# Gated linear attention inside 128 tokens: two coarse levels as rectangles, the fine levels as 32 by 32 diagonal blocks

## The chip, the core and the metric

The kernel runs on one core of a Trainium2 chip. The core has a matrix engine (TensorE, PE in the profile, with PEld for its weight loads), a vector engine (VectorE, DVE), a scalar engine (ScalarE, ACT), GpSimd (POOL) and SyncE (SP), which issues the large transfers. Each engine runs its own queue of instructions in order. The metric is the device time of one execution in microseconds: 1452.02 us, the median of three runs (1451.77 to 1452.31).

## The reference

The program is two blocks on 256 tokens of width 1024. The first block has two layers, each a mixer of three parts (sparse attention, gated linear attention, spatial gating) and a feed-forward part; the second block has banded attention and a mixture of 32 experts. The change touches only the gated linear attention, once in each of the two layers. It has 4 heads, 32 key channels and 64 value channels a head:

```python
def gla_mixer(q, k, v, a_lr, r, w_up, b_up, norm_g):
    ...
    g = jax.nn.log_sigmoid((a_lr @ w_up + b_up).astype(f32)).reshape(B, S, H, DK) / GLA_TAU
    ...
        bcum = jnp.cumsum(gc, axis=2)
        o_inter = jnp.einsum('bhck,bhkv->bhcv', qc * jnp.exp(bcum), state)
        diff = bcum[:, :, :, None, :] - bcum[:, :, None, :, :]
        decay = jnp.exp(jnp.where(causal[None, None, :, :, None], diff, -jnp.inf))
        attn = jnp.einsum('bhik,bhjk,bhijk->bhij', qc, kc, decay)
        o_intra = jnp.einsum('bhij,bhjv->bhiv', attn, vc)
    ...
    o = rmsnorm(o, norm_g) * jax.nn.silu(r.astype(f32)).reshape(B, S, H, DV)
```

So each pair of a query token and an earlier key token has a weight: the sum over 32 channels of q times k times the decay of that channel between the two tokens.

## The kernel before, in words

**The heads.** The kernel does the linear attention in two halves of 128 tokens (`tb`) instead of chunks of 64, and makes the weights inside a half by levels. At level s (64, 32, 16, 8, 4, 2, 1) the half is cut into blocks of 2s tokens; every query in a block's upper s tokens meets every key in its lower s tokens, and the decay is split at the middle of the block: the query carries the factor from the middle to itself, the key the factor from itself to the middle. A last level is the diagonal, where there is no decay. `_tables` (L75) makes the matrix of ones that sums the gates for all levels (`decay`), and the masks; `t_gla` (L1205) makes the exponentials `ex` and multiplies q and k into them. Any pair of tokens belongs to just one level.

`heads(hp)` (L1266) is started for two pairs of heads. Each of the eight levels is a full 128x128 product per head and half, with 32 channels on the rows of the matrix engine: four bursts of two levels (L1267 to L1282), 16 matmuls a pair in each, into two banks of PSUM, a bank for each head of the pair. After a burst, two predicated copies on DVE (L1285 to L1291), each 128 partitions by 512, put the places of one level into `at`. At the end two matmuls a pair make the weights between the two halves, and ACT copies them out. When both pairs are done, `t_gla` multiplies the weights with v, normalises and gates; its root is a power on POOL (`grs`), and a product with the norm's gains on POOL follows.

**What sets the order.** The large products with weights ("dense" here) run on the matrix engine as one stream: each weight tile of 128 rows is split into a high and a low part, by a cast on ACT (`whi`) and a subtraction on DVE (`wlo`), and multiplied three times. A scheduler (`step`, L443; `tick`, L466) places everything else between these products: it keeps a modelled clock for each engine, charges each instruction a price (`price`, L262), and lets the generators of the mixers go on one `yield` at a time, by rank, where their inputs are ready by the model. `heads` has rank 7 (L43). The order of all instructions is thereby fixed when the program is built. A change in what `heads` issues, or in its prices, moves its neighbours in all queues.

The neighbours of `heads` are, in each layer: the spatial gating (its norm is on DVE, an operation on 128x256), the compressed keys and values (`t_cmp`, L832: two products on DVE that move them out of PSUM, then six additions of 64x240 on POOL), the rotation of q on POOL (`t_qk`, L1031) and the copy of its transpose on DVE in two halves, then the attention over selected blocks and the window (`t_branch`, L1103), and the output projection (`w_out`, L1507), which is dense. All instructions pass through a recording helper, so that the profile shows one line for all, L258; tiles tell them apart. `arena`, `arena_o` and `arena_y` are the working memory of the mixers, `psum` the accumulators, `raw` the slots into which weights arrive.

Of the kernel before, what the change touches and what calls it, by code (L numbers as in the profile page):

```python
# [13 lines left out]
P = 128  # L14
# [60 lines left out]
def _tables():  # L75
    f = np.float32
    p, j = np.arange(P), np.arange(P)
# [45 lines left out]
    u, t = p[:, None], p[None]  # L123
    lev = [np.where(u >= t + 1, 1.0, 0.0)]
# [5 lines left out]
    lev.append(np.where(u <= t, 1.0, 0.0))  # L130
    t1.add("decay", np.stack(lev, 1) / 16.0)
    t1.add("tril", (j[None] <= p[:, None]) * 1.0)
    masks = []
    for s in (64, 32, 16, 8, 4, 2, 1):
        q, k = p[None], p[:, None]
        masks.append((q // (2 * s) == k // (2 * s)) & (q % (2 * s) >= s) & (k % (2 * s) < s))
    masks.append(p[None] == p[:, None])

    t2 = Tables()
    for name, dil, back in (("dist0", 1, 128), ("dist1", 4, 128), ("dist2", 16, 128), ("dist3", 1, 127)):  # L140
# [4 lines left out]


TABLES, WHERE, MASKS = _tables()


# [421 lines left out]
class Kernel:  # L571
# [633 lines left out]
    def t_gla(self, l):  # L1205
        nc, S = self.nc, self.side
        yield from S.wait(("ar", l), ("gqk", l), ("gv", l), ("par", l))
        qk = self.zs["gqk"]
        b = yield from S.get(1)
# [7 lines left out]
        for tb in range(2):  # L1217
# [11 lines left out]
            out=g16.rearrange("p a b -> p (a b)"), in0=pg, scalar=0.0, in1=ab, op0=ALU.min, op1=ALU.subtract  # L1229
# [5 lines left out]
        ex = yield from self.ar.new(8, 2, P)  # L1235
        for half in range(2):
            for tb in range(2):
                b = yield from S.get(1)
# [6 lines left out]
                    out=ex[:, half * 4 : half * 4 + 4, tb, :],  # L1245
                    in_=self.ps(b[0]).rearrange("p (a t) -> p a t", a=4),
# [7 lines left out]
        for i, s in enumerate((64, 32, 16, 8, 4, 2, 1)):  # L1254
            for tb in range(2):
                e = ex[:, i + 1 - tb, tb, :].rearrange("p (n r s) -> p n r s", r=2, s=s)
# [6 lines left out]
        at = yield from self.ar.new(4, 2, P)  # L1263
        ax = yield from self.ar.new(4, P)
        nc.gpsimd.memset(at, 0.0)
        def heads(hp):  # L1266
            for lp in range(4):  # L1267
                bs = yield from S.get(2)
                for ll in range(2):
                    lev = lp * 2 + ll  # L1270
                    for tb in range(2):
                        for e in range(2):
                            r = slice((hp * 2 + e) * 32, (hp * 2 + e) * 32 + 32)
                            if lev < 7:
                                a = c = ex[r, lev + 1 - tb, tb, :]
                            else:
                                a, c = qk[r, 1, tb * P : tb * P + P], qk[r, 0, tb * P : tb * P + P]
                            o = (ll * 2 + tb) * P
                            self.nc.tensor.matmul(
                                self.ps(bs[e])[:, o : o + P], lhsT=a, rhs=c, start=True, stop=True,  # L1280
                                skip_group_check=True, tile_position=((hp * 2 + e) * 32, 0),
                            )  # L1282
                yield
                two = self.psum[:, bs[0] : bs[1] + 1 : bs[1] - bs[0], :]
                for ll in range(2):  # L1285
                    lev = lp * 2 + ll
                    nc.vector.copy_predicated(
                        out=at[:, hp * 2 : hp * 2 + 2].rearrange("p a b c -> p a (b c)").rearrange("p a (b c) -> p a b c", b=2),
                        mask=self.masks[:, lev * P : lev * P + P].unsqueeze(1).unsqueeze(1).to_broadcast([P, 2, 2, P]),
                        data=two[:, :, ll * 256 : ll * 256 + 256].rearrange("p a (b c) -> p a b c", b=2),  # L1290
                    )  # L1291
                S.put(bs)
                yield
            bs = yield from S.get(2)
            for e in range(2):
                r = slice((hp * 2 + e) * 32, (hp * 2 + e) * 32 + 32)
                self.nc.tensor.matmul(
                    self.ps(bs[e])[:, 0:P], lhsT=ex[r, 0, 0, :], rhs=ex[r, 7, 1, :], start=True, stop=True,
                    skip_group_check=True, tile_position=((hp * 2 + e) * 32, 0),
                )  # L1300
            yield
            two = self.psum[:, bs[0] : bs[1] + 1 : bs[1] - bs[0], 0:P]
            nc.scalar.copy(out=ax[:, hp * 2 : hp * 2 + 2, :], in_=two)
            S.put(bs)
            yield

        for hp in range(2):
            S.start(heads(hp), ("gla_heads", l, hp), BLOCKS[l]["rank"]["heads"])
        yield from S.wait(("gla_heads", l, 0), ("gla_heads", l, 1))
        self.ar.drop(ex, qk)  # L1310
        b = yield from S.get(1)
        ps = self.ps(b[0]).rearrange("p (t h d) -> p t h d", t=2, h=4)
        for h in range(4):
# [22 lines left out]
            out=srn, in0=srn, in1=self.gln[:, l, :].unsqueeze(1).to_broadcast([P, 8, 64]), op=ALU.mult  # L1336
# [1333 lines left out]
```

## Time and profile before

| | before |
|---|---|
| median of 3 runs | 1452.02 us |
| profiled execution, its own time | 1452.91 us |
| span in the trace | 1451.1 us |
| PE busy, its share of the span | 1311.3 us, 90% |
| DVE busy | 724.6 us, 50% |
| ACT busy | 559.8 us, 39% |
| POOL busy | 215.9 us, 15% |
| moved by DMA | 360.21 MB, mean 248 GB/s |

The span is what the trace covers from first to last instruction; the execution's own time is 1.8 us more. Busy shares are means over the whole program. In layer 0 the bursts of the heads begin at 72.51 us, the attention's first matmul is at 103.33, PE has nothing but dense work from 143.1 to the feed-forward part at 163.4. In layer 1 the same stages begin at 410.30, 440.90 and 480.0 us.

Times are in microseconds from the start of the span, unless marked ns. The trace counts two PE instructions for a matmul on full float32 inputs, and one for the split products.

### The profile page before, as it was taken

To read this page: it belongs to the slowest core of one execution; us is meant where nothing else is said; L and a number is where in the kernel's file an instruction comes from. 1 tells how busy PE (TensorE), PEld (TensorE's weight loads), DVE (VectorE), ACT (ScalarE), POOL (GpSimd) and SP (SyncE) were. 2 spreads that over 40 slices of the span, in tenths; PEclk is the share of its full clock that TensorE was granted. 3 is DMA by queue.
4 is the path that set the end of the run, shared out by engine and by line. 5 is a ranking of instruction groups with operands and counts; after the bars stand their busy time and mean duration, and the time that the engine had idled before them with its cause. 6 is when DMAs were issued, how large, how long until landed. Compare 5 with 4: busy or idle time off the path is not lost.

```text
span 1451.1 us, 23004 instructions
## 1 busy us (share of the span) xinstructions
PE 1311.3 (90%) x8865; PEld 977.9 (67%) x8865; DVE 724.6 (50%) x1521; ACT 559.8 (39%) x1175; POOL 215.9 (15%) x345
## 2 busy tenths in 40 slices
PE   9989999999999999999999999998887777867665
PEld 8777999988777899988989899885332311412111
DVE  5586677765588677765676655563210200110001
ACT  5526555554536555545564546541110100100001
POOL 2154111101055011102442302010000000000000
PEclk9998999999999999999999999999989979988888
DMA  9651556555524465557435354688999999999995
GB/s 342 193 170 47 162 179 199 167 195 177 178 96 147 131 189 183 186 188 225 152 94 169 117 163 141 220 327 354 419 420 420 421 421 420 420 421 421 421 419 211
DMA packets 155076, 360.21 MB, mean 248 GB/s; under 512 B 8752, under 2 KB 98352, under 8 KB 130768
## 3 DMA queue, kind: packets, MB, share of 16 engines
q1 hardware_dynamic: 152928, 354.81, 66.8%
q0 software_dynamic: 1248, 3.11, 0.7%
q8 instruction: 71, 1.16, 0.3%
q10 hardware_dynamic: 784, 0.76, 0.2%
q14 instruction: 45, 0.37, 0.1%
HBM read 357.60 MB, written 1.05 MB: 247 GB/s over the span
## 4 chain that ended last, share of the span: by engine, by line
PE 41%; DMA 22%; DVE 3%; ACT 2%; POOL 1%; issue 1%; POOLq 0%; DVEq 0%; SPq 0%; ACTq 0%
PE psum L258 41%; DMA raw<-in_w_e_up_dram 8%; DMA raw_left<-in_w_e_down_dram 3%; DMA arena_y<-in_w_e_up_dram 3%; DMA raw<-in_w_e_down_dram 3%; DMA raw_right<-in_w_e_up_dram 3%; DMA raw_right<-in_w_e_down_dram 1%; DMA raw_left<-in_w_e_up_dram 1%; DVE arena L258 1%; ACT whi L258 1%; ACT arena L258 1%; DVE wlo L258 1%; POOL arena L258 1%; DVE arena_o L258 0%; ACT arena_o L258 0%
## 5 line engine op out<-in xcount | busy, mean ns | idle before, releaser
L258 DVE TENSOR_TENSOR wlo<-raw,whi 128x512 fp32r<-128x512 f32 (+3 forms) x552 | 397.2, 727 | 260.5 <-ACT whi L258 249.4
L258 ACT CAST whi<-raw 128x512 fp32r<-128x512 f32 (+3 forms) x552 | 332.8, 606 | 344.6 <-PE psum L258 274.4
L258 PE MATMUL psum<-h_hi,whi 128*128 128x256 f32 x1040 | 297.8, 286 | 3.0 <-ACT whi L258 3.0
L258 PE MATMUL psum<-h_lo,whi 128*128 128x256 f32 x1040 | 291.6, 280 | 0.1
L258 PE MATMUL psum<-h_hi,wlo 128*128 128x256 f32 x1040 | 290.2, 279 | 0.0
L258 PEld LDWEIGHTS psum<-h_hi,whi 128*128 128x128 f32 x1040 | 195.8, 188 | 10.1 <-issue 4.8
L258 PEld LDWEIGHTS psum<-h_lo,whi 128*128 128x128 f32 x1040 | 196.2, 189 | 0.9 <-issue 0.5
L258 PEld LDWEIGHTS psum<-h_hi,wlo 128*128 128x128 f32 x1040 | 196.0, 188 | 0.2 <-DVE wlo L258 0.2
L258 PE MATMUL psum<-raw,arena 128*32 128x512 f32 x608 | 164.0, 672 | 19.1 <-DMA raw<-in_w_e_up_dram 12.6
L258 PE MATMUL psum<-arena 64*128 64x128 f32 (+10 forms) x752 | 160.1, 418 | 21.6 <-DVE arena L258 8.2
L258 PE MATMUL psum<-whi,h_hi 128*128 128x256 f32 (+3 forms) x448 | 145.8, 325 | 1.4 <-ACT arena_o L258 1.1
L258 PE MATMUL psum<-whi,h_lo 128*128 128x256 f32 (+3 forms) x448 | 138.3, 309 | 0.0
L258 PE MATMUL psum<-wlo,h_hi 128*128 128x256 f32 (+3 forms) x448 | 138.3, 309 | 0.0
L258 PEld LDWEIGHTS psum<-arena 64*128 64x128 f32 (+4 forms) x752 | 73.1, 175 | 69.8 <-issue 23.7
L258 DVE SCALAR_TENSOR_TENSOR arena<-arena,psum 128x256 f32<-128x256 f32 (+2 forms) x36 | 17.8, 517 | 201.7 <-ACT arena L258 198.8
L258 PEld LDWEIGHTS psum<-raw,arena 128*32 128x32 f32 x608 | 34.4, 121 | 99.8 <-issue 60.3
L258 PE MATMUL psum<-raw_left,arena 128*32 128x512 f32 x400 | 81.2, 712 | 20.9 <-DMA raw_left<-in_w_e_gate_dram 14.8
L258 POOL TENSOR_TENSOR arena<-arena 128x512 f32<-128x512 f32 (+2 forms) x46 | 49.0, 1074 | 295.3 <-DVE arena L258 289.0
L258 PEld LDWEIGHTS psum<-whi,h_hi 128*128 128x128 f32 x448 | 85.3, 190 | 11.0 <-issue 4.4
L258 PEld LDWEIGHTS psum<-wlo,h_hi 128*128 128x128 f32 x448 | 85.4, 191 | 4.6 <-issue 1.4
L258 PEld LDWEIGHTS psum<-whi,h_lo 128*128 128x128 f32 x448 | 85.2, 190 | 4.5 <-DVE h_lo L258 0.2
L258 DVE COPY arena<-psum 128x384 f32<-128x384 f32 (+6 forms) x60 | 32.6, 543 | 108.0 <-ACT arena L258 95.7
(247 smaller groups left out, 1761.5 us busy)
## 6 DMA issues: line engine op xcount, KB each, us to landing
raw<-in_w_e_up_dram SPq DMA_DIRECT2D x32, 1024.0 KB, 19.8
raw<-in_w_in_dram SPq DMA_DIRECT2D x60, 512.0 KB, 4.9
raw<-in_w_e_gate_dram SPq DMA_DIRECT2D x24, 1024.0 KB, 19.8
raw<-in_w_gate_dram SPq DMA_DIRECT2D x44, 512.0 KB, 4.0
raw<-in_w_up_dram SPq DMA_DIRECT2D x44, 512.0 KB, 5.1
raw<-in_w_down_dram SPq DMA_DIRECT2D x20, 1024.0 KB, 5.2
raw_left<-in_w_e_gate_dram SPq DMA_DIRECT2D x20, 1024.0 KB, 19.9
raw<-in_w_e_down_dram SPq DMA_DIRECT2D x19, 1024.0 KB, 19.8
```

The costliest lines, as they stand in the source:

```text
L258: return f(*args, **kw)
```

## The change

The levels 64 and 32 become products of just the rectangles in which they count (64 by 64, and two of 32 by 32 a half), and ACT copies those to `at`. The five levels from 16 down and the diagonal lie wholly in the four diagonal blocks of 32 by 32 of a half; they become 32 by 32 products: 6 levels, 2 halves, 4 blocks and 2 heads, 96 matmuls for a pair of heads, all in one burst without a `yield`, into two banks. Six predicated copies of 128x128 a pair merge them by mask into a new tile `a32`, and four copies on ACT put its blocks onto the diagonal of `at`. The products between the halves go into the second burst. The mask table goes from 128x256 words to 128x48.

```diff
     masks = []
-    for s in (64, 32, 16, 8, 4, 2, 1):
+    q, k = np.arange(32)[None], p[:, None] % 32
+    for s in (16, 8, 4, 2, 1):
         masks.append((q // (2 * s) == k // (2 * s)) & (q % (2 * s) >= s) & (k % (2 * s) < s))
-    masks.append(p[None] == p[:, None])
+    masks.append(q == k)
...
         nc.gpsimd.memset(at, 0.0)
+        a32 = yield from self.ar.new(4, 2, 32)
+        nc.gpsimd.memset(a32, 0.0)
+
         def heads(hp):
-            for lp in range(4):
-                bs = yield from S.get(2)
-                for ll in range(2):
-                    lev = lp * 2 + ll
-                    for tb in range(2):
+            def one(bank, n, rows, e, a, c):
+                h = hp * 2 + e
+                r = slice(h * 32, h * 32 + 32)
+                nc.tensor.matmul(
+                    self.ps(bank)[rows[0] : rows[1], n : n + c.shape[-1]], lhsT=a[r], rhs=c[r], start=True, stop=True,
+                    skip_group_check=True, tile_position=(h * 32, rows[0]),
+                )
+
+            hs = slice(hp * 2, hp * 2 + 2)
+            bs = yield from S.get(2)
+            for i in range(6):
+                lev = 2 + i
+                for tb in range(2):
+                    if lev < 7:
+                        a = c = ex[:, lev + 1 - tb, tb, :]
+                    else:
+                        a, c = qk[:, 1, tb * P : tb * P + P], qk[:, 0, tb * P : tb * P + P]
+                    for o in range(0, P, 32):
                         for e in range(2):
...
+                            one(bs[e], (i * 2 + tb) * 32, (o, o + 32), e, a[:, o : o + 32], c[:, o : o + 32])
+            yield
+            two = self.psum[:, bs[0] : bs[1] + 1 : bs[1] - bs[0], 0:384].rearrange("p e (i t c) -> p e i t c", i=6, t=2)
+            for i in range(6):
+                nc.vector.copy_predicated(
+                    out=a32[:, hs],
+                    mask=self.masks[:, i * 32 : i * 32 + 32].unsqueeze(1).unsqueeze(1).to_broadcast([P, 2, 2, 32]),
+                    data=two[:, :, i],
+                )
+            S.put(bs)
+            yield
             bs = yield from S.get(2)
+            for tb in range(2):
+                x = ex[:, 1 - tb, tb, :], ex[:, 2 - tb, tb, :]
+                for e in range(2):
+                    one(bs[e], tb * 64, (0, 64), e, x[0][:, 0:64], x[0][:, 64:128])
+                for o in (0, 64):
+                    for e in range(2):
+                        one(bs[e], 128 + tb * 32, (o, o + 32), e, x[1][:, o : o + 32], x[1][:, o + 32 : o + 64])
             for e in range(2):
...
+                one(bs[e], 192, (0, P), e, ex[:, 0, 0, :], ex[:, 7, 1, :])
+            yield
+            two = self.psum[:, bs[0] : bs[1] + 1 : bs[1] - bs[0], :]
+            nc.scalar.copy(out=at[0:64, hs, :, 64:128], in_=two[0:64, :, 0:128].rearrange("p e (t c) -> p e t c", t=2))
+            for o in (0, 64):
+                nc.scalar.copy(
+                    out=at[o : o + 32, hs, :, o + 32 : o + 64],
+                    in_=two[o : o + 32, :, 128:192].rearrange("p e (t c) -> p e t c", t=2),
                 )
...
+            nc.scalar.copy(out=ax[:, hs], in_=two[:, :, 192:320])
             S.put(bs)
+            for o in range(0, P, 32):
+                nc.scalar.copy(out=at[o : o + 32, hs, :, o : o + 32], in_=a32[o : o + 32, hs])
             yield
```

The order of instructions changes in the two stretches of layers 0 and 1 alone; elsewhere it is the same. The queue of the matrix engine at the heads of layer 0, before (a row is a matmul with its output and inputs, the shape, and a count where it repeats; `arena_o` is where `ex` lies, the dense work reads `h` and `w`):

```order
L258 MATMUL psum<-arena_o 128x128 x16
L258 MATMUL psum<-h_hi,whi 128x256
...
L258 MATMUL psum<-whi,h_lo 128x256
L258 MATMUL psum<-arena_o 128x128 x16
L258 MATMUL psum<-whi,h_hi 128x280
```

And of the kernel after, at the same place:

```order
L259 MATMUL psum<-arena_o 32x32 x80
L259 MATMUL psum<-arena 32x32 x16
L259 MATMUL psum<-arena_o 32x32 x80
L259 MATMUL psum<-arena 32x32 x16
L259 MATMUL psum<-h_hi,whi 128x256
...
L259 MATMUL psum<-whi,h_lo 128x256
L259 MATMUL psum<-arena_o 64x64 x2
L259 MATMUL psum<-arena_o 32x32 x4
L259 MATMUL psum<-arena_o 64x64 x2
L259 MATMUL psum<-arena_o 32x32 x4
L259 MATMUL psum<-arena_o 128x128 x2
```

The first burst now holds all levels from 16 down for both pairs, and the second, twelve dense matmuls later, the rectangles and the product between the halves; the third to fifth bursts are gone.

DVE's queue at the same place, before. The TENSOR_SCALAR with `bnmv` and `bnrs` is the norm of the spatial gating, the two TENSOR_TENSOR with `rbc` move the compressed keys and values out of PSUM, those to `wlo` are weight splits:

```order
L258 TENSOR_SCALAR bnrs<-bnmv 128x2
L258 COPY_PREDICATED arena_o<-arena,psum 128x512 x4
L258 TENSOR_SCALAR arena_o<-arena_o,bnmv,bnrs 128x256 x2
L258 TENSOR_TENSOR arena_o<-psum,rbc 128x256 x2
L258 TENSOR_SCALAR arena_o<-psum,rstd 128x256
L258 TENSOR_TENSOR wlo<-raw_83,whi 128x280
L258 COPY_PREDICATED arena_o<-arena,psum 128x512 x4
L258 TENSOR_TENSOR wlo<-raw_83,whi 128x280 x2
```

After:

```order
L259 TENSOR_SCALAR bnrs<-bnmv 128x2
L259 COPY_PREDICATED arena<-arena,psum 128x128 x12
L259 TENSOR_SCALAR arena_o<-arena_o,bnmv,bnrs 128x256 x2
L259 TENSOR_TENSOR arena_o<-psum,rbc 128x256 x2
L259 TENSOR_SCALAR arena_o<-psum,rstd 128x256
L259 TENSOR_TENSOR wlo<-raw_83,whi 128x280 x3
L259 TENSOR_TENSOR wlo<-raw_81,whi 128x512 x4
```

All predicated copies of a layer now stand together, ahead of the norm, the two products and the splits.

POOL's queue behind the memsets of `heads`, before. The operations on 64x16x15 are the additions of the compressed keys and values, 128x16x32 is the rotation of q, the TENSOR_SCALAR with `rrb` are the scalings in the attention:

```order
L258 TENSOR_TENSOR arena_o<-arena_o,arena 64x16x15 x2
L258 MEMSET arena_o 128x16x2
L258 TENSOR_TENSOR arena_o<-arena_o,arena 64x16x15 x4
L258 TENSOR_TENSOR arena_o<-arena 128x16x32 x2
L258 TENSOR_TENSOR arena<-arena 128x4x32 x4
```

After; `grs` is the power that ends the norm of the linear attention, and the 128x512 the product with its gains:

```order
L259 TENSOR_TENSOR arena_o<-arena_o,arena 64x16x15 x2
L259 MEMSET arena_o 128x16x2
L259 TENSOR_TENSOR arena_o<-arena_o,arena 64x16x15 x2
L259 TENSOR_TENSOR arena_o<-arena 128x16x32 x2
L259 TENSOR_TENSOR arena_o<-arena_o,arena 64x16x15 x2
L259 TENSOR_TENSOR grs<-gss,tab_67 128x8
L259 TENSOR_TENSOR arena<-arena 128x512
```

The rotation moved ahead of two additions, and the end of the linear attention, which before stood behind the attention's first products, moved ahead of them. DVE's two products for it stand in the same way ahead of its copy of the second half of q's transpose. On PE, 12 dense matmuls of the output projection in layer 0 and 6 in layer 1 moved from behind the attention to between its parts: behind it 54 of one shape and 18 of another are left in layer 0 where 66 and 18 were, in layer 1 60 and 18.

## Rows read from the trace of the kernel before

**Rows 1.** The page's 40 equal slices of the span, busy tenths.
```profile
PE   9989999999999999999999999998887777867665
...
PEclk9998999999999999999999999999989979988888
DMA  9651556555524465557435354688999999999995
```
**Rows 2.** Stretches: us, busy time (count) by engine, granted clock, DMA share, GB/s.
```profile
core 0: us, PE busy (x) PEld busy (x) DVE busy (x) ACT busy (x) POOL busy (x), PEclk, DMA share, GB/s
72.50:103.30 30.80, 27.36 (x281) 21.55 (x280) 26.92 (x47) 7.11 (x14) 17.07 (x25) 0.89 0.44 138
103.30:143.10 39.80, 36.42 (x273) 28.98 (x270) 28.41 (x123) 23.54 (x86) 19.10 (x39) 0.87 0.25 80
143.10:163.40 20.30, 20.30 (x94) 16.69 (x93) 13.15 (x23) 11.78 (x24) 0.00 (x0) 1.00 0.50 156
410.30:440.90 30.60, 27.33 (x282) 21.40 (x281) 26.67 (x47) 7.59 (x15) 17.08 (x25) 0.89 0.43 139
440.90:480.00 39.10, 35.82 (x277) 29.07 (x274) 28.15 (x124) 23.66 (x87) 19.68 (x40) 0.91 0.31 97
```
**Rows 3.** PE's timeline, layer 0: start, us, tile, shapes, count, idle before.
```profile
72.51 1.72 PE L258 MATMUL psum<-arena_o 32*128 32x128 f32 x32
74.16 0.39 PE L258 MATMUL psum<-h_hi,whi 128*128 128x256 f32 x1
...
86.82 1.13 PE L258 MATMUL psum<-arena_o,arena 128*128 128x128 f32 x8 [2.07 <-DVE arena_o L258]
...
103.33 1.58 PE L258 MATMUL psum<-arena 64*128 64x128 f32 x16
...
105.63 1.72 PE L258 MATMUL psum<-arena 128*128 128x32 f32 x14
```
**Rows 4.** PE's timeline in the experts, column tiles of 32.
```profile
1004.54 0.62 PE L258 MATMUL psum<-raw,arena 128*32 128x512 f32 x1
1004.55 0.62 PE L258 MATMUL psum<-raw_right,arena 128*32 128x512 f32 x1
```
**Rows 5.** DVE's groups by shape: busy us, mean ns, idle before.
```profile
L258 DVE COPY_PREDICATED arena_o<-arena,psum 128x512 f32<-128x512 uint8 x32 | 22.8, 733 | 2.0 <-PE psum L258 1.4
...
L258 DVE TENSOR_TENSOR arena<-arena_y,g 128x128 f32<-128x128 f32 x16 | 4.5, 283 | 0.9 <-PE psum L258 0.8
```
**Rows 6.** DVE's timeline in the heads of layer 0.
```profile
74.75 2.87 DVE L258 COPY_PREDICATED arena_o<-arena,psum 128x512 f32<-128x512 uint8 x4
77.52 0.72 DVE L258 TENSOR_SCALAR arena_o<-arena_o,bnmv,bnrs 128x256 f32<-128x256 f32 x2
78.15 0.75 DVE L258 TENSOR_TENSOR arena_o<-psum,rbc 128x256 f32<-128x256 f32 x2
...
102.50 0.69 DVE L258 COPY arena<-psum 128x512 f32<-128x512 f32 x1 [0.71 <-PE psum L258]
```
**Rows 7.** POOL's timeline in layer 0.
```profile
74.89 0.73 POOL L258 TENSOR_TENSOR bnrs<-bnrs,tab 128x2 f32<-128x2 f32 x1 [9.39 <-DVE bnrs L258]
...
78.65 3.97 POOL L258 TENSOR_TENSOR arena_o<-arena_o,arena 64x240 f32<-64x240 f32 x4 [2.96 <-DVE arena_o L258]
...
88.72 3.41 POOL L258 TENSOR_TENSOR arena_o<-arena_o,arena 64x240 f32<-64x240 f32 x4
...
93.39 2.17 POOL L258 TENSOR_TENSOR arena_o<-arena 128x512 f32<-128x512 f32 x2 [1.25 <-issue]
...
118.18 2.02 POOL L258 TENSOR_TENSOR grs<-gss,tab 128x8 f32<-128x8 f32 x1 [4.71 <-DVE gss L258]
120.17 1.27 POOL L258 TENSOR_TENSOR arena<-arena 128x512 f32<-128x512 f32 x1
121.42 8.66 POOL L258 TENSOR_SCALAR arena_o<-arena_o,rrb 128x128 f32<-128x128 f32 x20
```
**Rows 8.** ACT's groups by shape: busy us, mean ns, idle before.
```profile
L258 ACT COPY arena<-psum 128x256 f32<-128x256 f32 x6 | 2.2, 367 | 2.3 <-PE psum L258 2.3
```

More of the change, by code (lines that the diff above doesn't have):

```diff
@@ L133, in _tables @@
     masks = []
-    for s in (64, 32, 16, 8, 4, 2, 1):
-        q, k = p[None], p[:, None]
+    q, k = np.arange(32)[None], p[:, None] % 32
+    for s in (16, 8, 4, 2, 1):
         masks.append((q // (2 * s) == k // (2 * s)) & (q % (2 * s) >= s) & (k % (2 * s) < s))
-    masks.append(p[None] == p[:, None])
+    masks.append(q == k)
     t2 = Tables()
@@ L1265, in t_gla @@
         nc.gpsimd.memset(at, 0.0)
+        a32 = yield from self.ar.new(4, 2, 32)
+        nc.gpsimd.memset(a32, 0.0)
         def heads(hp):
-            for lp in range(4):
-                bs = yield from S.get(2)
-                for ll in range(2):
-                    lev = lp * 2 + ll
-                    for tb in range(2):
-                        for e in range(2):
[L1273 to L1293, printed above, removed]
@@ L1294, in heads @@
-            bs = yield from S.get(2)
-            for e in range(2):
[L1296 to L1299, printed above, removed]
-                )
-            yield
-            two = self.psum[:, bs[0] : bs[1] + 1 : bs[1] - bs[0], 0:P]
-            nc.scalar.copy(out=ax[:, hp * 2 : hp * 2 + 2, :], in_=two)
+            def one(bank, n, rows, e, a, c):
[5 more added lines that the diff above has]
+                )
@@ L1309, in t_gla @@
         yield from S.wait(("gla_heads", l, 0), ("gla_heads", l, 1))
-        self.ar.drop(ex, qk)
+        self.ar.drop(ex, qk, a32)
         b = yield from S.get(1)
```

## The prediction

> **What bounds the kernel now.** I read the page's 40 slices first, then a table of stretches, then the timelines of PE, DVE and POOL in the stretch that the change touches. In the slices PE is busy at nine tenths or more for about two thirds of the span and the DMA engines take over in the last third [rows 1]. The edited code runs in the first part, once per layer. An instruction added to PE's queue there costs its full length unless PE waits anyway, and what is won there moves everything behind it, the transfers of the last third too, since those start when earlier weights free their slots.
>
> In each layer the edited code stands in a stretch where PE does wait. From the first burst of head matmuls to the attention (30.8 us in layer 0, 30.6 in layer 1) PE is busy 27.4 us, DVE 26.9, and the granted clock averages 0.89. In the attention stage behind it PE is busy 36.4 of 39.8 us at 0.87, in layer 1 35.8 of 39.1 at 0.91. Behind that PE runs dense at 1.00 [rows 2]. [...]
>
> **The change, part by part.** All times are layer 0's; layer 1 has the same order around the heads.
>
> *PE.* Before, a burst is 32 instructions (each fp32 matmul is two) of 128 columns for both head pairs; the first takes from 72.51 to the dense matmul at 74.16, 51.6 ns per instruction [rows 3]. Two heads use different rows of the array side by side, so one head's rows take 103 ns per instruction. After, the first burst holds 2 x 96 matmuls of 32 by 32, 384 instructions, and the second 28 matmuls, 56 instructions: 440 per layer for 136. No row shows a 32 by 32 tile with 32 columns. The bounds: a quarter of 51.6, 13 ns, if everything scales with the columns; 51.6 if nothing does. Below that, matmuls on different column groups start about 10 ns apart [rows 4], which would be 10 or less. Above, 14 instructions of 32 columns on full 128 by 128 tiles take 1.72 us, 123 ns each; there each loads weights of 128 columns, and a quarter of it is 31 [rows 3]. I take 26 ns, a quarter of the 103 of one head's rows: one stream at a time, with no side by side working between tiles. It lies midway, by ratio, between 13 and 51.6, and near the 31. So the first burst takes 384 x 26 ns = 10.0 us and ends at 82.5, with the last matmul through at 82.8.
>
> [...]
>
> *DVE.* Sixteen predicated copies of 128x512 per layer, 733 ns each, 11.7 us, become twelve of 128x128. A plain 128x128 operation takes 283 ns where 128x512 takes about 690 [rows 5, 6], so I take 0.3 us, 3.6 us in all. The 8 us saved lie on an engine busy 26.9 of 30.8 us [rows 2]. But they no longer wait for four small bursts: all twelve stand ahead of DVE's next work and wait for the 384 instructions. Queued behind them are the norm step of the spatial gating, the two products that move the compressed keys and values out of PSUM, and the weight splits; POOL waits for the products. Before, the products begin at 78.15 [rows 6] and POOL starts at 78.65 [rows 7].
>
> After: the burst's end 82.8, six copies of the second pair 1.8 (the first pair's lie beside PE), norm 0.72, first product 0.4: POOL starts at 85.8, 7.2 us later.
>
> *POOL to the attention.* POOL runs from 78.65 to 92.13 without a gap and starts the rotation of q at 93.39 [rows 7]. After, two of the additions (1.7 us, half of the 3.41 row) stand behind the rotation: 85.8 + 13.5 - 1.7 = 97.6, plus 2.17 = 99.8. Then 1.7 of additions, the power of 2.02 and the product of 1.27 that finish the gated attention, which before ran at 118.18 [rows 7]: 103.5 and 104.8. DVE's two products that wait for them stand ahead of its copy of the second half of q: 104.8 + 0.7 + 0.69 = 106.2. So the attention begins at 106.3, not 103.33 [rows 3]: **3.0 us later** in each layer, though the heads are done in two bursts. PE is not later than that: its 27.4 us here shrink by the old bursts (136 instructions, 7 us at 51.6) and the 3.4 us that the low clock costs, and grow by 12 us of new bursts and about 4 us of work moved in from the attention stage.
>
> *Attention stage.* The end of the gated attention leaves it: on POOL 3.3 us that stood ahead of 8.66 us of scalings (118.18 to 130.08) [rows 7], on DVE five 128x512-sized operations, on PE its twelve matmuls. In exchange 12 dense matmuls of the output projection move in (6 in layer 1). [...] I take 7 and 5.5 us back. [...]
>
> *Output projection.* 12 and 6 dense matmuls fewer behind the attention; 94 instructions take 20.30 us there [rows 2], 0.22 each: 2.6 and 1.3 us.
>
> *Small edits.* ACT gets 14 small copies more per layer, under 0.37 us each (a 128x256 copy takes that) [rows 8], at most 5 us on an engine busy 7.1 of 30.8 [rows 2]. They stand ahead of two weight casts, which PE needs only six takes later; if that cover is gone, a take waits about 1 us. The second memset on POOL is ahead of a wait of 9.39 us and costs nothing [rows 7]. The mask table shrinks by 0.1 MB: 0.1 us at the start at most.
>
> **The sum.** Layer 0: +3.0 - 7 - 2.6 = -6.6. Layer 1: +3.0 - 5.5 - 1.3 = -3.8. With the masks -10.5 us. The profiled execution took 1452.9 us (span 1451.1), the median is 1452.0, 0.9 less; against it the forecast is **1441.5 us**. Each nanosecond per instruction moves it by 2 x 0.384 = 0.77 us, so the sum is nothing at 40 ns.
>
> **Rivals.**
> [...]
> - *The stream of instructions sets the pace (slower).* The place is the first burst; the price 0.77 us per nanosecond; from 40 ns on it decides. At the 51.6 ns of before's burst [rows 3] the burst takes 19.8 us, POOL starts 17 us late, and the sum is -10.5 + 19.7 = +9.2: **1461**. [...] At the 123 ns of the full tiles it would be 1516. Against: before's burst is as long as its columns ask for, so it need not show any limit of the queue.
> - *The relief is hidden.* DVE's load in the heads falls, but the attention stage stays as long as its in-order engines make it, 1 us shorter: the sum loses 10.5 us and is 0, **1452**. For it: DVE is busy 28.4 us there and ACT 23.5 [rows 2], and POOL waits for DVE again and again. Against: what leaves the stage stands in the middle of POOL's and DVE's queues.
>
> **How the numbers follow.** Forecast 0.42, with its own range 1434 to 1449 (20 to 34 ns, 3 us either way in the stage); side by side 0.20; stream 0.25 (0.04 of it beyond 1470); hidden 0.13. Range for 8 in 10: from the side-by-side case, 1426, to just past the stream case at 52 ns, 1463. About 0.2%, 2.9 us, is what a measurement of this kernel tells from no change. Faster: 0.42 less 0.03, 0.20 and 0.02 of the hidden case, 0.61. Same: 0.02 and 0.09, 0.11. Slower: 0.28.
>
> **What would show it.** In the profile after: the burst of 384 instructions in each layer, its length over 384; DVE standing before the twelve copies until it ends; POOL's additions starting near 86 in layer 0; the attention's first matmul near 106; that stage some 33 us long with the clock nearer 1; the dense run behind it 2.6 us shorter; the rest shifted as a whole. [...]

## The result and the profile after

The kernel after takes 1479.07 us (median of 4 runs, 1476.46 to 1482.08), before 1452.16 (4 runs beside it): ratio 1.0184, interval 1.0172 to 1.0196. It is slower by 27 us, where 1441.5 was forecast and 1463 was the upper end.

The profiled execution took 1479.59 us. Its page has PE a little less busy than before (1308.1 us for 1311.3) in a longer span:

```profile
span 1477.8 us, 24273 instructions
...
PE 1308.1 (89%) x9473; PEld 973.4 (66%) x9473; DVE 713.6 (48%) x1513; ACT 566.6 (38%) x1203; POOL 220.2 (15%) x347
...
PE   8968899999977999999999999999877867866675
...
PEclk9988999999988999999999999999988979989878
```

The slices that fall most are the two stretches of the change; behind them the pattern of [rows 1] returns. The stretches of after, layer 0 in four pieces (the first burst, the dense work behind it, the rest up to the attention, the attention with the output projection), then layer 1 in two (heads; attention with projection):

```profile
71.50:82.68 11.18, 4.62 (x385) 4.24 (x385) 3.87 (x13) 0.42 (x1) 0.80 (x2) 0.69 0.27 97
82.68:95.40 12.72, 12.72 (x117) 11.77 (x112) 6.98 (x16) 8.47 (x24) 8.99 (x14) 0.74 0.07 7
95.40:112.80 17.40, 11.44 (x109) 8.07 (x107) 13.11 (x22) 3.93 (x8) 14.29 (x14) 0.91 0.72 239
112.80:174.80 62.00, 52.03 (x323) 38.03 (x320) 32.95 (x131) 28.94 (x97) 14.78 (x34) 0.91 0.24 73
426.60:462.58 35.98, 25.31 (x567) 21.85 (x565) 22.72 (x47) 12.40 (x32) 18.24 (x23) 0.79 0.27 89
462.58:520.96 58.38, 52.37 (x359) 38.33 (x356) 35.20 (x135) 29.39 (x97) 18.97 (x42) 0.92 0.39 123
```

The heads of layer 0 took 30.8 us before [rows 2] and take 41.3; PE is busy 4.62 of the first 11.18 us, and the dense work behind runs at a mean clock of 0.74. PE's timeline shows why, with the releaser of each wait in brackets:

```profile
71.49 1.94 PE L259 MATMUL psum<-arena_o 32*32 32x32 f32 x154
...
73.59 0.32 PE L259 MATMUL psum<-arena_o 32*32 32x32 f32 x14
78.28 1.53 PE L259 MATMUL psum<-arena_o 32*32 32x32 f32 x128 [4.37 <-issue]
82.00 0.30 PE L259 MATMUL psum<-arena_o 32*32 32x32 f32 x9 [2.19 <-issue]
...
82.68 0.58 PE L259 MATMUL psum<-h_hi,whi 128*128 128x256 f32 x1
...
109.88 1.12 PE L259 MATMUL psum<-tab,arena 128*128 128x128 f32 x4 [3.36 <-DVE arena L259]
...
112.80 1.77 PE L259 MATMUL psum<-arena 64*128 64x128 f32 x16
```

Where the tiles run, 128 of them take 1.53 us, 12 ns each. Between the runs PE waits 4.37 and 2.19 us for nothing that a semaphore would show ("issue"). The queue named "instruction" moves one packet of 16 KB ahead of each point where PE goes on, at 75.6 to 75.8 and at 79.2 to 79.4 us, some 2.6 us earlier both times; this is its row, with the data's above it, from 75 to 78 us:

```profile
q1 hardware_dynamic: 174, 0.32, 27.9%
q8 instruction: 1, 0.02, 2.2%
```

From 78 to 82 us there is again one, and it is the only packet of any queue, so that other transfers do not explain the second wait. From 65 to 75 the instruction queue moves none.

DVE and POOL stand as forecast, up to POOL's start:

```profile
73.88 1.98 DVE L259 COPY_PREDICATED arena<-arena,psum 128x128 f32<-128x128 uint8 x6
82.79 1.99 DVE L259 COPY_PREDICATED arena<-arena,psum 128x128 f32<-128x128 uint8 x6 [6.93 <-PE psum L259]
...
109.75 0.68 DVE L259 COPY arena<-psum 128x512 f32<-128x512 f32 x1
```

```profile
85.83 4.07 POOL L259 TENSOR_TENSOR arena_o<-arena_o,arena 64x240 f32<-64x240 f32 x4 [11.15 <-DVE arena_o L259]
...
99.13 3.78 POOL L259 TENSOR_TENSOR arena_o<-arena 128x512 f32<-128x512 f32 x2 [2.18 <-PE psum L259]
102.99 2.54 POOL L259 TENSOR_TENSOR arena_o<-arena_o,arena 64x240 f32<-64x240 f32 x2
105.71 1.96 POOL L259 TENSOR_TENSOR grs<-gss,tab 128x8 f32<-128x8 f32 x1 [0.18 <-DVE gss L259]
```

POOL starts at 85.83 (85.8 was forecast). What follows takes longer than in [rows 7]: the rotation of q stands 2.18 us waiting for PE and takes 3.78 us where it took 2.17.

### The profile page after: what moved, and what is told of

It is laid out like the page before. It is cut to its first block, busy times and chain, and to the rows that moved or that the text cites. A ratio compares the mean times of both kernels' runs of the same rounds, so it can differ in the third digit from the quotient of the medians.

```text
span 1477.8 us, 24273 instructions
## 1 busy us (share of the span) xinstructions
PE 1308.1 (89%) x9473; PEld 973.4 (66%) x9473; DVE 713.6 (48%) x1513; ACT 566.6 (38%) x1203; POOL 220.2 (15%) x347
## 4 chain that ended last, share of the span: by engine, by line
PE 60%; DMA 26%; ACT 5%; DVE 4%; issue 2%; POOL 2%; POOLq 0%; ACTq 0%; DVEq 0%; SPq 0%
PE psum L259 60%; DMA raw<-in_w_e_up_dram 8%; DMA raw_left<-in_w_e_up_dram 4%; DMA raw_left<-in_w_e_down_dram 4%; DMA raw_right<-in_w_e_up_dram 4%; DMA raw_right<-in_w_e_down_dram 3%; ACT whi L259 2%; DVE wlo L259 2%; DMA arena_y<-in_w_e_up_dram 1%; DMA raw<-in_w_e_down_dram 1%; DVE arena L259 1%; ACT arena L259 1%; ACT arena_o L259 1%; POOL arena L259 1%; POOL arena_o L259 1%
## 5 line engine op out<-in xcount | busy, mean ns | idle before, releaser
L259 DVE TENSOR_TENSOR wlo<-raw,whi 128x512 fp32r<-128x512 f32 (+3 forms) x552 | 401.9, 735 | 270.3 <-ACT whi L259 259.8
L259 PEld LDWEIGHTS psum<-whi,h_hi 128*128 128x128 f32 x448 | 85.8, 192 | 9.9 <-issue 4.0
L259 PE MATMUL psum<-tab,arena 128*128 128x128 f32 (+4 forms) x306 | 52.9, 300 | 42.1 <-DVE arena L259 36.4
L259 PEld LDWEIGHTS psum<-wlo,h_hi 128*128 128x128 f32 x448 | 85.9, 192 | 4.6 <-issue 1.4
L259 PEld LDWEIGHTS psum<-whi,h_lo 128*128 128x128 f32 x448 | 85.8, 192 | 4.6 <-DVE h_lo L259 0.2
```

What stands on the lines that cost most here:

```text
L259: return f(*args, **kw)
```

## How the layers are compared

Each layer is cut at three instructions that every kernel here has: the first matmul of the heads, the first of the attention (64x128), and the first sum of squares for the feed-forward norm, which for before and after is

```profile
158.41 0.60 PE L258 MATMUL psum<-tab,x 128*128 128x128 f32 x4
...
494.30 0.60 PE L258 MATMUL psum<-tab,x 128*128 128x128 f32 x4
```

```profile
174.81 0.60 PE L259 MATMUL psum<-tab,x 128*128 128x128 f32 x4
...
520.96 0.60 PE L259 MATMUL psum<-tab,x 128*128 128x128 f32 x4
```

The table has the lengths between them in us, from each kernel's trace ("heads", then "attention" with the output projection), what is left behind the last cut, and the time with its ratio to before.

| kernel | layer 0 | layer 1 | behind | median, ratio (interval) |
|---|---|---|---|---|
| before | 30.8 + 55.1 | 30.6 + 53.4 | 956.8 | 1452.2 |
| after | 41.3 + 62.0 | 35.9 + 58.4 | 956.8 | 1479.1, 1.0184 (1.0172 to 1.0196) |
| e1_before_tiny | 39.8 + 55.0 | 38.4 + 52.3 | 957.3 | 1468.3, 1.0109 (1.0092 to 1.0126) |
| e2_after_quarter | 37.5 + 62.4 | 32.5 + 58.5 | 956.4 | 1472.9, 1.0132 (1.0115 to 1.0149) |
| e3_after_split | 39.6 + 60.4 | 35.9 + 56.6 | 961.2 | 1482.2, 1.0202 (1.0185 to 1.0219) |
| e4_before_tiny2 | 50.4 + 56.2 | 52.9 + 53.4 | 957.7 | 1495.1, 1.0276 (1.0252 to 1.0299) |
| e5_new_in_old_order | 27.2 + 58.8 | 27.0 + 59.2 | 961.5 | 1460.2, 1.0059 (1.0046 to 1.0072) |
| e6_new_heads_own_room | 27.2 + 56.9 | 28.2 + 58.0 | 960.4 | 1457.5, 1.0047 (1.0033 to 1.0060) |
| e7_after_old_room | 41.7 + 52.8 | 43.6 + 51.5 | 957.0 | 1472.2, 1.0148 (1.0135 to 1.0161) |
| e8_after_tail_later | 38.4 + 65.0 | 38.6 + 57.9 | 957.9 | 1482.8, 1.0214 (1.0194 to 1.0233) |
| e9_after_old_room_quarter | 35.5 + 52.8 | 40.0 + 51.6 | 957.0 | 1464.6, 1.0091 (1.0074 to 1.0108) |
| e10_blocks64 | 27.3 + 55.6 | 29.6 + 57.8 | 960.6 | 1456.3, 1.0023 (1.0013 to 1.0032) |
| e11_old_order_pad | 27.2 + 58.7 | 27.1 + 59.1 | 957.5 | 1466.2, 1.0098 (1.0082 to 1.0115) |
| e12_blocks64_pad | 27.3 + 55.6 | 27.3 + 56.0 | 957.1 | 1449.9, 0.9988 (0.9978 to 0.9997) |

After's 26.7 us of span (1477.8 less 1451.1) are 17.4 in layer 0 (103.3 for 85.9) and 10.3 in layer 1 (94.3 for 84.0), less 1.0 at the start.

## The experiments

**The stream alone, in the old order.** e1 adds the first burst's tiles to the kernel before, uncharged by the scheduler, so that nothing else moves:

```diff
+                for i in range(96 if lp == 0 else 0):
+                    h, o, n = hp * 2 + i % 2, i // 2 % 4 * 32, i // 8 % 12 * 32
+                    a = ex[h * 32 : h * 32 + 32, 2, 0, o : o + 32]
+                    nc.nc.tensor.matmul(
+                        self.ps(bs[i % 2])[o : o + 32, n : n + 32], lhsT=a, rhs=a, start=True, stop=True,
...
```

> The kernel before, its order on every engine kept, with 96 matmuls of 32x32 for each head pair put ahead of the first burst of the heads in both layers (192 a layer, 384 PE instructions); their sums are overwritten by the burst and nothing reads them. Theory F (fetch): the price of the change is the PE queue running out of instructions, which come in by DMA in pieces, at about 29 ns per instruction over the burst, and the low clock behind it. Then the first burst takes about 11 us more, with two idle stretches of 2 to 4 us put down to issue, and the time is 1471 to 1482. Theory O (order): the time went into the new order of the attention's steps; then this kernel, which keeps the old order, hides much of the burst in PE's waits there and stays below 1465.

e4 doubles them (192 for 96).

> As the first kernel of this set, with twice the unread matmuls (384 a layer, 768 PE instructions). Theory F: each 128 further matmul instructions with their weight loads cost one more wait for a piece, 3.7 us, so the burst takes 11 us more than in the first kernel and the time is 18 to 26 us above it. If the waits were a single event at the start of the burst (a piece that happened to be late), the further 384 instructions would run at 13 ns and cost 5 us a layer, 10 us in all.

e1 took 16 us more than before, between what the two theories said. Its burst has the two waits of after:

```profile
78.33 1.53 PE L1272 MATMUL psum<-arena_o 32*32 32x32 f32 x128 [3.62 <-issue]
82.06 0.84 PE L1272 MATMUL psum<-arena_o 32*32 32x32 f32 x59 [2.20 <-issue]
```

In layer 0 the dense work behind the first burst starts 13.2 us after the burst's begin (71.62 to 84.84) where it was 1.65, so 11.6 us later; the heads grow by 9.0 us, and by 7.8 in layer 1, so only some 2.6 us are hidden. The attention, in its old order, is 0.1 and 1.1 us shorter. e4 takes 27 us more than e1, just past the upper end of what fetching said (18 to 26): the wait comes again and again, four times in layer 0 (4.71, 1.93, 2.47 and 2.20 us). How the program comes in is counted on the pages: the instruction queue's row reads, before and in e4,

```profile
q8 instruction: 71, 1.16, 0.3%
```

```profile
q8 instruction: 83, 1.36, 0.4%
```

These are twelve packets more for 1536 instructions and as many weight loads: 256 entries of PE's program a packet. 128 tiles with their loads are one packet by this count, and the run between the two waits of layer 0 has 128 in after and in e1. In after it took 3.7 us from that run to the next (78.28 to 82.00), where its tiles were through in 1.53.

**The order alone.** e2 keeps after's order and takes away three of four instructions of the first burst; one product of 128 by 32 stands for four blocks, so that three blocks of each four hold other values than the reference's:

```diff
-                    for o in range(0, P, 32):
-                        for e in range(2):
-                            one(bs[e], (i * 2 + tb) * 32, (o, o + 32), e, a[:, o : o + 32], c[:, o : o + 32])
+                    for e in range(2):
...
+                        nc.nc.tensor.matmul(
+                            self.ps(bs[e])[:, n : n + 32], lhsT=a[r], rhs=c[r, 0:32], start=True, stop=True,
...
```

> The kernel after, with its order on every engine, but the four 32x32 blocks of a level, half and head are made by one matmul of 128 by 32 (all keys, the queries of the first block), so that the burst has 48 matmuls instead of 192 a layer; the blocks past the first hold other products than the reference's. Theory F: no idle stretch in the burst, POOL's additions some 9 us earlier, the clock stays up behind it, and the time falls to 1440 to 1455. Theory O: the order is as in the kernel after, so the attention stage stays long; the time falls by less than 10 us, to 1470 or above.

No wait for issue is left in the burst, yet only 6 us came back: the stream is not the whole cause, and fetching alone had said 1440 to 1455. The attention stays at 62.4 and 58.5 us, as in after. Two things keep e2 from undoing the burst. Its wider products take 5.6 us (72.14 to 77.70), not before's 1.7 [rows 3]. And the clock behind it does not stay up, as was expected; these are the burst and the dense work behind it in layer 0:

```profile
72.14:77.70 5.56, 5.56 (x97) 5.50 (x96) 3.88 (x13) 0.42 (x1) 0.80 (x2) 0.90 0.56 192
77.70:90.00 12.30, 12.30 (x93) 10.90 (x92) 5.87 (x15) 6.76 (x21) 8.56 (x14) 0.50 0.00 1
```

PE was busy all through this burst, and the dense work runs at 0.50, lower than after's 0.74 behind a burst full of waits. So in e2 the low clock came behind a burst without waits. What set it is open: behind e9's burst, the same products, it is 0.85 in layer 0 and 0.50 in layer 1.

**Spread out.** e3 puts a yield behind each level of the burst.

```diff
                             one(bs[e], (i * 2 + tb) * 32, (o, o + 32), e, a[:, o : o + 32], c[:, o : o + 32])
-            yield
+                yield
```

> The kernel after with a yield behind each of the six levels of the first burst, so that dense work comes between bursts of 64 PE instructions. Theory F: the instructions arrive in time, no idle stretch over 1 us in the tiles, and the time is 1440 to 1460. Theory O: the tiles' price hardly matters, the order of the attention does; it changes here too, so a time above 1465 would speak for O, one below for either.

It is no faster, where fetching had said 1440 to 1460: two waits of 1.71 and 1.80 us for issue are left in layer 0, the order is another one again, and 4 us are lost at the far end (below). A time above 1465 was to speak for the order, but with an order of its own and waits left it separates little.

**The new products in the old order.** e5 deals the levels out to before's four bursts, charges the scheduler as before, and lays the block tile into `ax`, which is there anyway; every engine's order is then before's. e6 differs by the block tile's own room and the mask table's old room given back, and by four copies on ACT that then stand behind the copy to `ax` instead of ahead of it:

```diff
-        a32 = ax[:, :, 0:64].rearrange("p h (t c) -> p h t c", t=2)
+        a32 = yield from self.ar.new(4, 2, 32)
...
-        masks = new(256)[:, 0 : MASKS.shape[1]]
+        masks = new(MASKS.shape[1])
```

> The 32x32 products and rectangles of the change, but in the order of the kernel before on every engine: the four bursts of the heads now hold two, two, one and one of the fine levels, the fifth the rectangles and the products between halves, each step charged to the scheduler as before; the block tile lies in memory that is taken anyway, so that the memory plan is that of before too. Theory O (order): the change's loss beyond the stream of tiles comes from the order, so this kernel has none of it, and DVE's 8 us a layer are saved: 1440 to 1454. Theory F (fetch): 440 PE instructions a layer still have to come in within 15 us of heads; 2 to 6 us of idle a layer, 1452 to 1465.

> The kernel of the first run of this set, with its heads in the same order, but with the block tile in a room of its own and the mask table's old room given back, as in the changed kernel. Only the memory plan differs, and through it the order of the attention's steps behind the heads. If the memory plan is what moved the attention, this is 5 to 14 us slower than the first run of the set; if the number of yields in the heads is, it is within 3 us of it.

Here DVE's relief is seen: the heads of e5 take 27.2 us for 30.8, with DVE busy 19.0 for 26.9, though one wait of 3.07 us for issue is left. But the attention gives it back, in the same order, at a clock of 0.83 for 0.91; these are e5's two stretches, and before's attention with its projection:

```profile
71.54:98.73 27.19, 23.02 (x562) 18.46 (x561) 18.98 (x44) 8.91 (x21) 16.45 (x25) 0.94 0.46 148
98.73:157.48 58.75, 55.61 (x364) 44.86 (x360) 37.60 (x138) 33.17 (x108) 18.91 (x38) 0.83 0.32 99
```

```profile
103.33:158.41 55.08, 51.70 (x339) 41.49 (x336) 37.37 (x138) 31.24 (x101) 19.07 (x39) 0.91 0.32 101
```

0.08 of 58.75 us would be 4.7 us of clock (an estimate), enough for the 3.7 us that the stage grew; why the clock stays low there is open. e5's time lies where fetching had it (1452 to 1465), above what the order alone would give (1440 to 1454). e6's median is 3 us below e5's, with intervals that overlap, not 5 to 14 above it: in this order a room of its own costs nothing.

**The memory plan in the new order.** e7 is after with the edits above the other way round, the place of the four copies on ACT too.

> The changed kernel (one burst, its yields) with the memory plan of the kernel before: the block tile in memory that is taken anyway. If the memory plan moved the attention to its loss, this falls from 1479 to 1460 to 1468, which leaves the stream of tiles alone; if the yields did, it stays at 1474 or above.

It took 7 us less than after, and lies between what the two theories said (1460 to 1468; 1474 or above). The attention of layer 0 falls from 62.0 to 52.8 us, that of layer 1 from 58.4 to 51.5, while layer 1's heads grow by 7.6; by whole layers, 8.9 us come back in layer 0 and none in layer 1 (95.0 for 94.3). The clearest difference is where the selection of the blocks stands. Before, PE comes to it thus:

```profile
117.35 0.24 PE L258 MATMUL psum<-tab,arena 32*128 32x32 f32 x1 [0.36 <-DVE arena L258]
```

After, it comes to it and to the last attention product thus:

```profile
135.82 0.24 PE L259 MATMUL psum<-tab,arena 32*128 32x32 f32 x1 [0.71 <-DVE arena L259]
...
156.31 1.93 PE L259 MATMUL psum<-tab,arena_o 128*128 128x128 f32 x6 [2.95 <-POOL arena_o L259]
```

and in e7:

```profile
125.95 0.25 PE L259 MATMUL psum<-tab,arena 32*128 32x32 f32 x1 [0.42 <-DVE arena L259]
...
141.83 1.69 PE L259 MATMUL psum<-tab,arena_o 128*128 128x128 f32 x6 [0.83 <-POOL arena_o L259]
```

In after the selection is 23.0 us behind the start of the attention, in e7 12.6, before 14.0. In DVE's queue stand ahead of the selection's operations (32x64) the row maxima of 14 branch products in after, of 10 in e7 and of 13 before. What after has more than before is four weight splits of the output projection, which moved in there, and they waited 5.73 us in all for casts that on ACT stand behind the exponentials of the same branches (e7: two splits, 1.19 us; before: none). The longest of these waits, and the selection behind them:

```profile
127.00 0.69 DVE L259 TENSOR_TENSOR wlo<-raw,whi 128x512 fp32r<-128x512 f32 x1 [2.69 <-ACT whi L259]
...
134.87 0.40 DVE L259 TENSOR_TENSOR arena<-psum,arena 32x64 f32<-32x64 f32 x3
```

What hangs on the selection then came last, with little beside it:

```profile
148.60:158.00 9.40, 5.73 (x40) 3.51 (x38) 3.32 (x16) 3.53 (x13) 1.62 (x4) 0.98 0.01 2
```

That the memory plan decides is shown; that the late selection is how, is argued. The clock is a part of it: the attention and its projection run at 0.97 and 1.00 in e7 for 0.91 and 0.92 in after, which would be 3.7 and 4.7 us of the 9.2 and 6.9 (an estimate, 0.06 of 62.0 us and 0.08 of 58.4). And in e7's layer 1 heads the dense work behind the burst runs at 0.50 throughout,

```profile
429.40:441.00 11.60, 11.60 (x89) 10.20 (x89) 5.43 (x14) 6.53 (x21) 8.26 (x13) 0.50 0.01 1
```

where after has 0.87 (437.8 to 449.4): 4.3 of the 7.6 us by which those heads grew (an estimate, 0.37 of 11.60 us). So that layer 1 gets nothing back does not show that the plan costs nothing there.

**The tail held back.** e8 is e7 with the end of the linear attention behind q's transposes, as before the change.

```diff
+        yield from S.wait(("qT", l))
         ss = self.small([P, 8], "gss")
```

> The changed kernel with the memory plan of before (1472), and the end of the gated linear attention (its root, its products) held back until the transposes of q are done, as it was before the change. Theory T (tail): what the heads stage lost beyond the stream of tiles is this tail, which stands ahead of the attention's first products on POOL and DVE; then the attention begins 4 to 6 us earlier in each layer and the time is 1460 to 1467. Rival: the tail only fills a wait for the stream and its slow clock; then the attention begins at the same time and the time stays at 1469 to 1474.

The attention begins 3.2 and 5.0 us earlier, near what the theory had; then it takes 12.2 and 6.4 us more, and the time is 11 us above e7, outside what either theory said. Moving the tail back gains nothing in this order. e8 also bounds the reading of e7: its selection comes early, 11.3 us behind the start of the attention (121.34 on DVE, start 110.07), and its stage is the longest of layer 0, 65.0 us. A late selection is not the only way in which an order lengthens the stage.

**Both losses out.** e9 is e7 with e2's edit.

> The changed kernel with the memory plan of before (1472), with one 128 by 32 product for four blocks, so a quarter of the instructions in the first burst, every order kept; the blocks past the first hold other products than the reference's. If the fetching of instructions costs what the kernel of before with unread tiles showed (15 us for 384 instructions a layer), less the 5.5 us that these wider products themselves take for a burst, this gives back 5 to 6 us of burst a layer and some of the clock: 1458 to 1465. If only the order matters, 1469 to 1474.

It came in as expected and gives back 7.6 us, all in the heads (6.1 and 3.5 in the trace), so the stream acts in the new order as in the old. Read against e2 it is also the memory plan's edit a second time: the attention falls from 62.4 to 52.8 and from 58.5 to 51.6 us, as from after to e7.

**Fewer instructions, and the far end.** e10 is e5 with blocks of 64 (levels 32 down, two blocks a half), 64 PE instructions a burst for 128; e11 is e5 and e12 is e10 with 32 unread small matmuls at the program's start, in e12 on tiles of 32 by 32:

```diff
+        for i in range(32):
+            o = i % 4 * 32
+            nc.nc.tensor.matmul(
+                self.ps(6)[o : o + 32, i // 4 * 2 : i // 4 * 2 + 2], lhsT=self.ones[0:32, 0:32], rhs=self.ones[0:32, 0:2],
...
```

> The idea of the change with blocks of 64 by 64 for all levels from 32 down, in the order and with the memory plan of the kernel before: 64 PE instructions a burst for both pairs instead of 128, 14 predicated copies of 128x256 a layer. Fetch: fewer instructions, no idle stretch over 1 us in the heads, DVE saves about 5 us a layer; 1446 to 1454. If the attention gives the gain back through the clock as in the run with the old order, 1451 to 1456.

> The run with the new products in the old order (1460), with 32 further two-column matmuls, 128 entries of PE's program, at the program's start, where PE waits for data; nothing else differs. That run lost 4.7 us of its 8 at the far end of the program, where PE idles 6.2 us for issue behind a branch. If that comes from where the branch falls in the pieces in which PE's program is fetched, the idle is gone with the shift and the time is 1454 to 1457; if not, it stays at 1459 to 1461.

> The run with blocks of 64 in the old order (1456), with 32 further unread tiny matmuls, 128 entries of PE's program, at the program's start, on 32 by 32 tiles so that they take under 2 us where PE waits for data. That run too idled 5.7 us for issue behind the branch near the end. If the idle hangs on where the branch falls in the fetched pieces, it is gone here, and the time is 1450 to 1453, the change's idea without its losses; the gain of DVE's relief is then still given back in the attention. If it does not hang on that, the time stays at 1455 to 1458.

e10 has no wait for issue in its heads. Its time is at the upper end of the second case (1451 to 1456). Both e5 and e10 lose some 4 us in the last 40 us of the program, where a branch jumps over a part that runs only when an expert gets too many tokens: PE stands 6.18 and 5.66 us there for issue. This is e5, then e11 and e12:

```profile
1424.80 6.59 PE L258 MATMUL psum<-raw,arena 128*32 128x512 f32 x32 [6.18 <-issue]
```

```profile
1430.80 1.94 PE L258 MATMUL psum<-raw,arena 128*32 128x512 f32 x6 [0.88 <-PEq L2361]
```

```profile
1414.55 2.12 PE L258 MATMUL psum<-raw,arena 128*32 128x512 f32 x6 [0.77 <-PEq L2353]
```

In e11 the wait is gone (957.5 us behind the last cut for 961.5), but its padding ran on full tiles and took 11.1 us at the start, so its time missed what was expected. In both pairs half a packet of entries more at the front of the program took some 4 us off its end (4.0 and 3.5). e12, with the wait gone, is the one kernel here that is not slower than before: 0.12% faster (0.03 to 0.22%), less than the 0.2% that the prediction counts as a change. Between e10 and e12 layer 1 differs by 4.2 us too, in the same order; these are the attention and its projection there, in e10 and in e12:

```profile
437.21:494.99 57.78, 54.44 (x347) 43.78 (x344) 37.52 (x138) 31.93 (x103) 19.56 (x39) 0.85 0.30 93
```

```profile
434.71:490.68 55.97, 52.02 (x348) 41.98 (x344) 37.46 (x138) 32.04 (x103) 19.57 (x39) 0.91 0.35 113
```

So e12's lead over e10 is the far end and the clock, and no run tells what moved the clock.

## Why the prediction was wrong

**Right.** The burst's cost: 384 instructions in 11.19 us (71.49 to 82.68) are 29 ns each for the 26 forecast. That is luck: the mechanism was another one than one stream at a time, 12 ns an instruction with two waits between. The copies took 303 ns for 0.3 us. POOL started at 85.83 for 85.8, which rests on the same luck. The dense work behind the burst ran at a mean clock of 0.74, for which the sum has no term.

**Small edits.** ACT's small copies did hold up more than was said: DVE waited 5.38 us for a cast that stood behind them (87.17 to 91.89 on ACT).

```profile
92.37 5.73 DVE L259 TENSOR_TENSOR wlo<-raw,whi 128x280 fp32r<-128x280 f32 x6 [5.38 <-ACT whi L259]
```

PE was busy all the time from 82.68 to 95.40 and did not wait for it, and no run isolates what it cost.

**The step "POOL to the attention" failed.** It has the attention 20.5 us behind POOL's start; it came 27.0 behind, 6.5 us more. The sum took the durations of before, followed POOL alone and said that PE is not later. PE was later. POOL was done with its additions at 96.96 and then stood 2.18 us for PE, which was busy without a gap from the burst's last run at 82.00 to 98.99, most of it dense work at a clock of 0.74 (12.72 us, of which 0.26 would be 3.3 lost, an estimate). So the rotation starts 1.5 us behind the forecast (99.13 for 97.6). It then takes 1.6 us longer than in [rows 7], and the additions behind it 0.8 us longer (2.54 for 1.7); DVE is busy beside them, but it was beside the rotation before too, so why is open. Behind DVE's copy at 109.75 stood transposes and products in PE's own queue, another 2.4 us, which the sum left out. With 0.2 us of small waits these are the 6.5. That the path through PE's first burst has so little slack, e1 shows: in the old order, with nothing else changed, 11.6 us more ahead of the dense work made the heads longer by 9.0. In after the burst is 9.5 us longer than before and the heads 10.5; the forecast had 8.3 and passed on 3.0.

**The step "Attention stage" failed in sign, in both layers.** It forecast 7 and 5.5 us back, and 2.6 and 1.3 more in the projection; stage and projection together came out 6.9 and 5.0 longer. No run shows the 7 and 5.5 us. What before's trace shows of the stage in layer 0 is 3.4 us in which PE is not busy [rows 2] and a clock of 0.50 from 118.7 to 128.8 us, 1.00 ahead of it and behind it. The reading that work leaves the stage was sound: in e7 stage and projection are 2.3 and 1.9 us shorter than before. What was not looked at is the order inside the stage. The new block tile and the smaller mask table change which memory is free, the scheduler puts other work ahead, and the selection comes 9 us later in its stage; e7, which gives that room back, takes 8.9 us out of layer 0. In layer 1 its stage is 6.9 us shorter too, but its heads, with the dense work behind the burst at 0.50 for 0.87, are 7.6 longer. What makes up 3.6 of layer 1's 10.3 us, beyond the 6.7 that e1 measures for the stream there, is open.

So layer 0's 17.4 us match the stream's 8.9 (e1, with the clock behind its burst) and the memory plan's 8.9 (e7, with the clock of its stage), which leave about nothing for DVE's relief and the tail. No run has both undone at before's burst length; e9, with a burst of 5.1 us and the old plan, has 88.3 us in layer 0 where before has 85.9.

**The rivals.** "The stream of instructions sets the pace" had the right end and place, not the size: it needed 40 ns an instruction to decide and got 29. The 29 are not the tiles' own pace: in after's run of 128 they took 12 ns each, close to the 13 that the prediction had for tiles that scale with their columns, and 6.56 of the burst's 11.19 us are the waits of 4.37 and 2.19 us for issue. 12 ns is the pace of tiles side by side, the case with 0.20 of the chances; with the waits and the order after is slower all the same. The wait for issue is not the burst's alone: at the jump near the end PE stood 6.18 us in e5.

## What to carry to other kernels

Count program entries, not only columns: here PE got through a packet of 256 entries in 1.53 us, the next run started 3.7 us behind the start of that one, and the burst of 384 instructions took 11.19 us with 4.37 and 2.19 us of waits. Count the clock behind it too: the dense work that followed such bursts here ran at 0.74 in after and, with no wait in the burst, at 0.50 in e2. When a scheduler and a shared memory plan fix the order, a new tile is an edit to every queue: compare the order far behind the change too, and try the change in the old order first. On a path where PE's waits look like cover, find what the wait is for before you spend it.

## What was not expected of the hardware

- Tiles of 32 by 32 with 32 columns in float32 ran at 12 ns per instruction in after's run between two waits (128 in 1.53 us).
- PE's program came in packets of 256 entries (12 more in e4 than before, for 3072), and where PE stood for issue in after's first burst its runs started 3.7 us apart (78.28 and 82.00).
- Behind a burst of 32-row products in which PE was busy throughout (5.56 us in e2), 12.3 us of dense work ran at 0.50.
- Behind the jump near the program's end PE's wait was 6.18 us in e5 and 0.88 in e11, 5.66 in e10 and 0.77 in e12; e11 and e12 have 128 entries more at the program's start.
- The same order ran at two clocks: layer 1's attention at 0.85 in e10 and 0.91 in e12, 1.8 us apart.
